# Block sums of a Strassen-type FFN made piece by piece ahead of time, and the last item's rows ordered behind its sums

## Chip, cores, metric

One Trainium2 chip, one core. The metric is the device time of one execution in microseconds (us); three executions of the kernel before were timed, and one more was profiled.

## What is computed

One pre-norm residual layer on x (2048 tokens x 1024 channels, float32). Cut to what matters here:

```python
h = rms_norm(x, mix_norm_g) @ w_in                 # q, k, v, forget gates, z
merged = concat(rms_norm(forgetting_attention(q, k, v, log_f)), rms_norm(spatial_gating(gelu(z))))
x = x + merged @ w_out
xn = rms_norm(x, ffn_norm_g)
gate, up = split(xn @ w_gate_up)                   # 1024 x 2*2816
x = x + (silu(gate) * up) @ w_down                 # 2816 x 1024
out = rms_norm(x, final_norm_g)
```

The change lies in the last three lines, the FFN and the final norm.

## The kernel before

Everything is float32 in and out. To multiply with float32 precision, each operand is split into a high and a low half (a ScalarE cast at L129 and a VectorE subtraction at L132), and each product is three matmuls: high x high, high x low, low x high.

The kernel runs through the input projection, attention with the gating MLP beside it, the output projection, and then the FFN, which starts about 1095 us into the profiled execution. The FFN has five stages: stages 1 and 2 are the up projection (`Up`, gate and up together) for the two halves of the tokens, 22 items each; stages 3, 4 and 5 are the down projection (`Down`) for three ranges of the hidden dimension, 8 items each, an item being 256 tokens. Each item is a two by two block product in the Winograd form: seven products n = 0 to 6 instead of eight. An item's seven left operands are streamed: loaded into `raw` tiles, added and subtracted (L1352, from `stream`) and split into `wh` and `wl` tiles, of which there are six each (`NW`). The seven right operands of a stage stay in place in SBUF for the whole stage, as high and low halves (`R`, some of them stored in tiles that are also named `wh` and `wl`). They are four raw blocks b11, b12, b21, b22 of the right matrix and three block sums made with four additions over 128 x 2048 elements (128 x 1536 in stage 5).

Items are taken in groups of two (`grp`; the last two items of stage 5 are groups of one). In a group, product n of both items runs, then their evacuation (`it.evac(n)`: sums from PSUM into SBUF on VectorE, ScalarE and GpSimd), then n + 1. In the last group of stages 1 to 4, after product n has been done for the last time, the resident operand n is rewritten for the next stage (`refill`, `keep_as`). The four raw blocks of the next stage (`staged`) are loaded ahead into the tiles `sg0` to `sg3`, and the block sums are made in those tiles, by VectorE but for one on GpSimd: one sum before the last group, three within it, between the splits:

```python
        yield keep(0, b11)
        tt(te[1], b11, b11, b12, ALU.add)
        yield keep(1, b11)
        yield keep(2, b21)
        tt(te[2], b21, b21, b11, ALU.subtract)
        tt(te[3], b11, b22, b11, ALU.subtract)
        yield keep(3, b11)
```

In stage 5 an item's two rows of tiles (t = 2 tp and 2 tp + 1) are finished with their last sums: `done` (L1517) squares the row on ScalarE, makes 1/sqrt on VectorE and GpSimd (`rsqrt`, L175 and L177), scales the row on VectorE (L1540) and stores it. These are generators in the list `posts`; the main loop takes a step of the first of them after each product of an item. The last item but for its second row goes a shorter way (t = 14, L1523 to L1533): half of its squares are taken early.

Each engine works its queue in order, and so does SyncE (SP), which issues nearly all loads and stores here. The order in a queue is set when the program is built by a list scheduler: the order of the program is the priority, and what is ready earlier by its own reckoning can go ahead of its place. `with behind(i):` places what is traced in the block after i on i's engine. The loads of attention's first operands are placed in this way after stores of the last chunk of the input projection (L1221 to L1229).

Of the kernel before, what the change touches and what calls it, by code (L numbers as in the profile page):

```python
# [8 lines left out]
F32 = mybir.dt.float32  # L9
F32R = mybir.dt.float32r  # L10
AF = mybir.ActivationFunctionType
ALU = mybir.AluOpType
# [4 lines left out]
P = 128  # L17
S = 2048
D = 1024
# [6 lines left out]
CH = 512  # L26
# [25 lines left out]
KB = [8, 8, 6]  # L52
NF_ = 6
RL = 2
SQ = 'p'
TE = ['vvvv', 'vvpv', 'vvvv', 'vvvv', 'vvvv', 'vvpv']
SE = 'pvpv'
NY = 4
NR = 5
# [27 lines left out]
def trunk(ctx: ExitStack, tc: tile.TileContext, x, x_t, mix_g, w_in, b_f, ln_g, ln_b, w_st, b_st, on_g, w_out,  # L87
# [85 lines left out]
    def rsqrt(p, ss, scale, tag, n=1):  # L173
        a = T(p, [P, n], F32, tag + "a")
        nc.vector.tensor_scalar(a, ss, scale, EPS, ALU.mult, ALU.add)  # L175
        r = T(p, [P, n], F32, tag + "r")
        nc.gpsimd.tensor_tensor(r, a, mhalf[:, 0:n], ALU.pow)  # L177
        return r
# [1149 lines left out]
    def stage():  # L1328
        return [T(pers, [P, 4, CH], F32, f"sg{n}") for n in range(4)]

    def staged(s):

        sg = stage()
        for i, t in enumerate(sg):
            if s < 3:
                ld(t, XT[s - 1][i])
                continue
            kh, r0 = KB[s - 3] // 2, sum(KB[: s - 3])
            r0 = (r0 + (i // 2) * kh) * P
            ld(t[:, 0:kh, :],  # L1340
               w_down[r0 : r0 + kh * P, (i % 2) * CH : (i % 2 + 1) * CH].rearrange("(k p) n -> p k n", p=P))
        return sg

# [5 lines left out]
    JOIN = {2: 0, 6: 3}  # L1349

    def tt(e, o, a, b, op):
        (nc.vector if e == "v" else nc.gpsimd).tensor_tensor(o, a, b, op)  # L1352

    def keep_as(i, src, kh=4):
        rh, rl = resident(i)
        hi_of(nc.scalar, rh[:, 0:kh, :], src)
        lo_of(nc.vector, rl[:, 0:kh, :], src, rh[:, 0:kh, :])
        return rh, rl

    def refill(sg, kh, te):  # L1360

        b11, b12, b21, b22 = (t[:, 0:kh, :] for t in sg)

        def keep(i, src):
            return keep_as(i, src, kh)

        yield keep(0, b11)
        tt(te[1], b11, b11, b12, ALU.add)
        yield keep(1, b11)
        yield keep(2, b21)  # L1370
        tt(te[2], b21, b21, b11, ALU.subtract)
        tt(te[3], b11, b22, b11, ALU.subtract)
        yield keep(3, b11)
        yield keep(4, b12)
        yield keep(5, b21)
        yield keep(6, b22)

    def stream(a11, a12, a21, a22):

# [17 lines left out]
    class Rows:  # L1397
# [10 lines left out]
        def evac(self, n):  # L1408
            ps = self.ps
            if n == 0:  # L1410
                self.x = self.rows()
                for m in range(2):
                    ld(self.x[m], self.source(2 * self.tp + m))
                self.u = T(pev, [P, CH], F32, "u", bufs=NU)
            x = [[self.x[m][:, c * CH : (c + 1) * CH] for c in range(2)] for m in range(2)]
            u = self.u
            if n == 0:
                copies.append(nc.scalar.copy(u, ps[0]))  # L1418
            elif n == 1:
                nc.vector.tensor_tensor(u, u, ps[1], ALU.add)  # L1420
                tt(self.adder, x[0][1], x[0][1], u, ALU.add)
            elif n == 2:
                nc.vector.tensor_tensor(x[0][0], x[0][0], ps[2], ALU.add)
            elif n == 3:
                nc.vector.tensor_tensor(x[1][1], x[1][1], ps[3], ALU.add)
            elif n == 4:
                nc.vector.tensor_tensor(u, u, ps[4], ALU.add)
                tt(self.adder, x[1][1], x[1][1], u, ALU.add)
            elif n == 5:
                nc.vector.tensor_tensor(x[1][0], x[1][0], ps[5], ALU.add)  # L1430
                tt(self.adder, x[1][0], x[1][0], u, ALU.add)
            elif n == 6:
                nc.vector.tensor_tensor(x[0][1], x[0][1], ps[6], ALU.add)
            for m in {5: (1,), 6: (0,)}.get(n, ()):
                posts.append(self.done(2 * self.tp + m, self.x[m], now[0]))

    class Up:
# [17 lines left out]
        def evac(self, n):  # L1455
            ps = self.ps
            if n == 0:
                self.h = T(pev, [P, 2, CH], F32, "hT", bufs=NH)
                self.u = T(pev, [P, CH], F32, "u", bufs=NH)
                self.c = T(pev, [P, CH], F32, "c", bufs=NH)  # L1460
            h0, h1, u, c = self.h[:, 0, :], self.h[:, 1, :], self.u, self.c
            if n == 0:
                nc.scalar.copy(u, ps[0])
            elif n == 1:
                nc.vector.tensor_tensor(u, u, ps[1], ALU.add)
            elif n == 2:
                nc.scalar.activation(h0, ps[2], AF.Silu)
            elif n == 3:
                nc.vector.tensor_tensor(c, u, ps[3], ALU.add)
            elif n == 4:  # L1470
                nc.vector.tensor_tensor(c, c, ps[4], ALU.add)
                nc.vector.tensor_tensor(h1, u, ps[4], ALU.add)
            elif n == 5:
                nc.vector.tensor_tensor(h1, h1, ps[5], ALU.add)
                nc.gpsimd.tensor_tensor(h0, h0, h1, ALU.mult)
            elif n == 6:
                nc.vector.tensor_tensor(u, u, ps[6], ALU.add)
                nc.scalar.activation(h1, u, AF.Silu)
                nc.gpsimd.tensor_tensor(h1, h1, c, ALU.mult)
                kb, r = [(i, j) for i in range(3) for j in range(KB[i])][self.fi]  # L1480
                ld(HD[kb][self.half * 8 : (self.half + 1) * 8, :, r, :].rearrange("b p t -> p b t"),
                   self.h.rearrange("p q (b t) -> p (q b) t", t=P))

    class Down(Rows):
        def __init__(self, kb, tp):
# [14 lines left out]
        def source(self, t):  # L1500
            return XA[t]
# [15 lines left out]
        def done(self, t, xt, at):  # L1517
            if self.kb < 2:
                ld(XA[t], xt)
                return  # L1520
            ss = T(pev, [P, 1], F32, "ss4")
            o = out[t * P : (t + 1) * P, :]
            if t == NB - 2:  # L1523
                right = xt[:, CH:]
                self.squares(right, ss)
                nc.vector.scalar_tensor_tensor(ss, ss, 1.0 / D, self.a, ALU.mult, ALU.add)  # L1526
                r = T(pev, [P, 1], F32, "r4r")
                nc.gpsimd.tensor_tensor(r, ss, mhalf[:, 0:1], ALU.pow)  # L1528
                nc.vector.scalar_tensor_tensor(right, right, r, finb[:, CH:], ALU.mult, ALU.mult)  # L1529
                ld(o[:, CH:], right)  # L1530
                nc.scalar.activation(xt[:, 0:CH], xt[:, 0:CH], AF.Copy, scale=r)
                ld(o[:, 0:CH], xt[:, 0:CH])
# [6 lines left out]
            r = rsqrt(pev, ss, 1.0 / D, "r4")  # L1539
            nc.vector.scalar_tensor_tensor(xt, xt, r, finb, ALU.mult, ALU.mult)  # L1540
            ld(o, xt)
            yield
# [88 lines left out]
    make()  # L1631
    load(1)
    nextR = [None] * 7
    for q in range(len(slots)):
        p, n = slots[q]
        s, i, its, last = grp[p]
        if n == 0 and i == 0 and s > 1:
            R, nextR = nextR, [None] * 7
            if s == 5:
                finb = T(pers, [P, 4, CH], F32, "sg0")[:, 0:2, :].rearrange("p a n -> p (a n)")  # L1640
                ld(finb, fin_g.rearrange("(o n) -> o n", o=1).broadcast_to([P, D]))
        if n == 0 and i == 2 and s < 5:
            sg = staged(s + 1)
        last = last and s < 5
        if n == 4 and s < 5 and i + 2 * len(its) == len(sets[s - 1]):
            b = [t[:, 0 : sets[s][0].kh, :] for t in sg]
            tt(TE[s + 1][0], b[1], b[3], b[1], ALU.subtract)
        if n == 0 and last:
            fill = refill(sg, sets[s][0].kh, TE[s + 1])
        while nq < len(slots) and len(made) + len(grp[slots[nq][0]][2]) <= LW:  # L1650
            make()
        if n == 0:
# [18 lines left out]
                it.evac(m)  # L1671
        if n == 0:
            now[0] = p
        for _ in range(len(its)):
            while posts and next(posts[0], 0) == 0:
                posts.pop(0)
        if last:
            nextR[n] = next(fill)
    finish(posts)
    estk.close()  # L1680

# [43 lines left out]
```

## Time and profile before

| | us |
|---|---|
| median of 3 runs | 2375.95 |
| lowest and highest | 2375.18, 2379.35 |
| profiled execution | 2381.17 |
| its span, first to last instruction | 2379.4 |
| TensorE (PE) busy in the span | 2340.1 |
| VectorE (DVE) busy | 1669.8 |
| ScalarE (ACT) busy | 1055.7 |
| GpSimd (POOL) busy | 623.3 |

The profiled execution is 5.22 us over the median. Sums are made against the profiled execution, and 1.77 us of it lie outside the span. A row of a timeline has the start, the duration, the engine, the line, the operation, the tiles (out <- in) and, in brackets, how long the engine had been idle before it and what ended that. A row of waits has the total, the times and the longest. A row of windows has the length of the window and then the busy time of each engine.

### The profile page before, as it was taken

What the parts mean: (1) busy time and instruction counts of PE and PEld (TensorE: products, weight loads), DVE (VectorE), ACT (ScalarE), POOL (GpSimd) and SP (SyncE); (2) the same over time, 40 slices, a digit from 0 to 9 for tenths busy, and PEclk for the clock granted to TensorE, in tenths of its full rate; (3) what the DMA queues carried; (4) which work ended last, traced back from release to release, by engine and by line L of the source; (5) the groups of instructions that cost most, each with busy time, mean ns of one, the idle gap of its engine ahead of it and who ended that gap; (6) DMA issues with size and microseconds to landing.
All of it is one profiled execution on the core that took longest, in us unless ns stands there. A gap on an engine that the chain in (4) does not pass through costs nothing. (4 is left out here: it accounts for less than half of the span.)

```text
span 2379.4 us, 31425 instructions
## 1 busy us (share of the span) xinstructions
PE 2340.1 (98%) x10582; PEld 1894.4 (80%) x10582; DVE 1669.8 (70%) x2736; ACT 1055.7 (44%) x1770; POOL 623.3 (26%) x705
## 2 busy tenths in 40 slices
PE   9999999999999989999999999999999999999997
PEld 7778777777777768788888888788888878888886
DVE  6658668888888666467655656965555696696888
ACT  5322138777787766344323233432323242332433
POOL 1100012122121222221323323232322325354531
PEclk9999999999999999999999999999999999999999
DMA  8845667655687865666233232423232245455453
GB/s 271 284 154 193 205 206 207 180 161 156 191 211 237 223 206 168 216 214 199 71 89 92 80 94 76 151 83 89 72 89 82 80 141 186 167 186 200 152 190 148
DMA packets 358152, 380.60 MB, mean 160 GB/s; under 512 B 22292, under 2 KB 275924, under 8 KB 355432
## 3 DMA queue, kind: packets, MB, share of 16 engines
q1 hardware_dynamic: 342008, 335.36, 46.6%
q0 software_dynamic: 7616, 27.33, 3.3%
q10 hardware_dynamic: 8368, 15.91, 1.8%
q8 instruction: 85, 1.39, 0.3%
q14 instruction: 75, 0.61, 0.1%
HBM read 253.35 MB, written 125.18 MB: 159 GB/s over the span
## 5 line engine op out<-in xcount | busy, mean ns | idle before, releaser
L129 ACT CAST wh<-raw 128x512 fp32r<-128x512 f32 (+2 forms) x492 | 302.1, 621 | 748.3 <-PE pp L1663 608.3
L132 DVE TENSOR_TENSOR wl<-raw,wh 128x512 fp32r<-128x512 f32 (+2 forms) x496 | 373.2, 762 | 82.0 <-ACT wh L129 81.5
L1663 PE MATMUL pp<-wl,wh 128*128 128x512 f32 x1056 | 325.4, 389 | 1.2 <-ACT u L1418 1.0
L1663 PE MATMUL pp<-wh,wh 128*128 128x512 f32 x1056 | 325.4, 389 | 0.0
L1352 POOL TENSOR_TENSOR raw<-raw 128x512 f32<-128x512 f32 (+1 forms) x124 | 163.6, 1321 | 510.0 <-DMA raw<-in_w_gu_dram 357.9
L132 DVE TENSOR_TENSOR Pl<-Pt,Ph 128x512 fp32r<-128x512 f32 (+1 forms) x320 | 195.2, 615 | 80.4 <-ACT Ph L129 77.5
L1663 PEld LDWEIGHTS pp<-wl,wh 128*128 128x128 f32 x1056 | 198.1, 188 | 43.0 <-ACT u L1418 1.4
L1663 PEld LDWEIGHTS pp<-wh,wh 128*128 128x128 f32 x1056 | 198.2, 188 | 41.2
L738 ACT ACTIVATE Pt<-mx_ps 128x512 f32<-128x512 f32 (+1 forms) x320 | 169.2, 533 | 124.9 <-PE mx_ps L736 120.7
L1663 PE MATMUL pp<-wl,wl 128*128 128x512 f32 x528 | 205.8, 390 | 1.0 <-DVE wl L132 1.0
L1663 PE MATMUL pp<-wh,wl 128*128 128x512 f32 x528 | 205.4, 389 | 0.0
L927 PE MATMUL z<-wh,xz 128*128 128x512 f32 x496 | 188.9, 397 | 0.0
L1352 DVE TENSOR_TENSOR raw<-raw,raw 128x512 f32<-128x512 f32 (+1 forms) x112 | 132.1, 1181 | 77.7 <-POOL raw L1352 74.2
L129 ACT CAST Ph<-Pt 128x512 fp32r<-128x512 f32 (+1 forms) x320 | 175.9, 557 | 19.3 <-PE tp L770 3.8
L363 DVE TENSOR_REDUCE mx<-mx_ps 128x1 f32<-128x512 f32 x192 | 129.9, 682 | 20.5 <-PE mx_ps L361 20.0
L748 POOL TENSOR_SCALAR_AFFINE_SELECT Ph<-Ph 128x128 fp32r<-128x128 f32 x128 | 52.8, 413 | 314.4 <-DVE Pl L132 219.6
L768 PE MATMUL tp<-Ph,V 128*128 128x512 f32 (+1 forms) x320 | 118.8, 371 | 3.7 <-POOL Ph L748 2.6
L735 PE MATMUL mx_ps<-A,D 74*128 74x512 f32 (+1 forms) x320 | 119.3, 373 | 2.9 <-ACT Pt L738 2.9
L361 PE MATMUL mx_ps<-D,A 66*128 66x512 f32 (+2 forms) x320 | 118.6, 373 | 2.6 <-issue 2.0
L773 PE MATMUL tp<-Pl,V 128*128 128x512 f32 (+1 forms) x320 | 118.6, 370 | 1.3 <-POOL Pl L748 0.9
L736 PE MATMUL mx_ps<-B,C 128*128 128x512 f32 (+1 forms) x320 | 117.5, 368 | 0.0
L1663 PEld LDWEIGHTS pp<-wl,wl 128*128 128x128 f32 x528 | 99.1, 188 | 22.6 <-DVE wl L132 2.1
(340 smaller groups left out, 5301.7 us busy)
## 6 DMA issues: line engine op xcount, KB each, us to landing
raw<-in_w_gu_dram SPq DMA_DIRECT2D x88, 512.0 KB
xz<-XS SPq DMA_DIRECT2D x31, 1024.0 KB
HD<-hT SPq DMA_DIRECT2D x44, 512.0 KB
D<-KH SPq DMA_DIRECT2D x112, 128.0 KB
XA<-xa SPq DMA_DIRECT2D x27, 512.0 KB
raw<-HD SPq DMA_DIRECT2D x24, 512.0 KB
XA<-xb SPq DMA_DIRECT2D x21, 512.0 KB
xa<-XA SPq DMA_DIRECT2D x20, 512.0 KB
```

The lines of the kernel that those rows point to most:

```text
L129: return nc.scalar.copy(o, i) if eng is nc.scalar else eng.tensor_copy(o, i)
L132: return eng.tensor_tensor(o, i, f(h), ALU.subtract)
L361: last_mx.append(nc.tensor.matmul(pm[:, 0:n], lhs, Dt[0 : lhs.shape[0], 0:n], start=True, stop=True))
L363: nc.vector.tensor_reduce(mx[:, a, s : s + 1], pm, AX.X, ALU.max)
L735: nc.tensor.matmul(st[:, off:], Dt[:, b * P : (b + 1) * P], A[:, off:], start=True, stop=False)
L736: nc.tensor.matmul(st[:, off:], C[:, b * P : (b + 1) * P], B[:, off:], start=False, stop=True)
L738: nc.scalar.activation(Pt[:, off:], st[:, off:], AF.Exp)
L768: nc.tensor.matmul(pv[:, off:], V[:, 0:P], Ph[:, off:], start=kb == 0, stop=False)
L773: nc.tensor.matmul(pv[:, off:], V[:, 0:P], Pl[:, off:], start=False, stop=kb == 4 * j + 3)
L927: nc.tensor.matmul(pz, xz[a][:, k, :], w[b][:, k, :], start=n == 0, stop=n == 3 * KT - 1)
L1352: (nc.vector if e == "v" else nc.gpsimd).tensor_tensor(o, a, b, op)
L1663: nc.tensor.matmul(pm, a[:, k, :], b[:, k, :], start=on is None and k == 0 and e == 0, stop=k == it.kh - 1 and e == 2, skip_group_check=n ...
```

## The change

The four wide sums of a stage (the table `TE`, the calls in `refill` and the one before the last group) are gone. A generator `block_sums` makes them instead in one piece per group, for 15 groups from the second group of stage 1 on (4 pieces for each of stages 2, 3 and 4, 3 for stage 5): four loads of 128 x 512 into two `xa` tiles after product 3, two VectorE sums after product 5 and two after product 6, and two stores into a DRAM buffer `SM` after product 2 of the next group. Loads and stores stand behind the last store of hidden rows (`hd`) in SP's queue. The resident operands are then loaded ready made: n = 0, 2 and 6 from the source, n = 1, 3, 4 and 5 from `SM`, the first four into `sg0` to `sg3` at item 14 of 22 in stages 1 and 2 and at item 2 of 8 in stages 3 and 4, the other three into `sg0` to `sg2` within the last group, each as soon as the operand that lay there has been split.

In the last group of all, the steps of `posts` are taken two at a time after products 0 to 3, none after 4 and one after 5 and 6, and from product 1 on they are placed behind the item's last sum of that product (`it.last`). The scaling of row 15 is moved behind all of row 14's steps.

The change was described in a few words as "Attention's first operands loaded during the last chunk, together with block sums made a piece per group and the last item's rows behind each product's sums". No line of the diff touches attention or the input projection.

```diff
-TE = ['vvvv', 'vvpv', 'vvvv', 'vvvv', 'vvvv', 'vvpv']
...
+    SM = {s: T(dram, [P, 4, 4, CH], F32, f"SM{s}") for s in (2, 3, 4, 5)}
+    def source(s, n):
+        if n in (0, 2, 6):
+            return block(s, {0: 0, 2: 2, 6: 3}[n])
+        return SM[s][:, {1: 0, 4: 1, 5: 2, 3: 3}[n], 0 : sets[s - 1][0].kh]
+    def fetch(s, n):
+        t = T(pers, [P, 4, CH], F32, f"sg{n % 4}")[:, 0 : sets[s - 1][0].kh]
+        ld(t, source(s, n))
+        return t
+    hd = []
+    def block_sums():
+        last = None
+        for s in (2, 3, 4, 5):
+            for k in range(sets[s - 1][0].kh):
+                n = yield
+                while n != 2:
+                    n = yield
+                if last:
+                    with behind(hd[-1]):
+                        put(*last)
+                while n != 3:
+                    n = yield
+                t = [T(xap, [P, D], F32, "xa") for _ in range(2)]
+                b = [t[i // 2][:, (i % 2) * CH : (i % 2 + 1) * CH] for i in range(4)]
+                with behind(*hd[-1:]):
+                    for i in range(4):
+                        ld(b[i], block(s, i)[:, k])
+                while n != 5:
+                    n = yield
+                tt("v", b[1], b[3], b[1], ALU.subtract)
+                tt("v", b[0], b[0], b[1], ALU.add)
+                n = yield
+                tt("v", b[2], b[2], b[0], ALU.subtract)
+                tt("v", b[3], b[3], b[0], ALU.subtract)
+                last = s, k, t
...
-    def refill(sg, kh, te):
...
+    def refill(s, sg):
+        kh = sets[s - 1][0].kh
+        for n in range(7):
+            r = keep_as(n, sg[n], kh)
+            if n < 3:
+                sg.append(fetch(s, n + 4))
+            yield r
...
             r = rsqrt(pev, ss, 1.0 / D, "r4")
+            if at == len(grp) - 1:
+                yield
             nc.vector.scalar_tensor_tensor(xt, xt, r, finb, ALU.mult, ALU.mult)
...
-        if n == 0 and i == 2 and s < 5:
-            sg = staged(s + 1)
+        if n == 0 and i == max(2, len(sets[s - 1]) - 8) and s < 5:
+            sg = [fetch(s + 1, m) for m in range(4)]
...
-        for _ in range(len(its)):
-            while posts and next(posts[0], 0) == 0:
-                posts.pop(0)
+        tail = p == len(grp) - 1
+        with behind(*[its[0].last] if tail and n else ()):
+            for _ in range((2, 2, 2, 2, 0, 1, 1)[n] if tail else len(its)):
+                while posts and next(posts[0], 0) == 0:
+                    posts.pop(0)
+            if tail and n == 6:
+                next(posts.pop(), None)
         if last:
             nextR[n] = next(fill)
+        if sums and p:
+            try:
+                sums.send(n)
+            except StopIteration:
+                sums = None
```

More of the change, by code (lines that the diff above doesn't have):

```diff
@@ L1329, in stage, with block @@
         return [T(pers, [P, 4, CH], F32, f"sg{n}") for n in range(4)]
+    def block(s, i):
+        if s < 3:
+            return XT[s - 1][i]
+        kh, r0 = KB[s - 3] // 2, sum(KB[: s - 3])
+        r0 = (r0 + (i // 2) * kh) * P
+        return w_down[r0 : r0 + kh * P, (i % 2) * CH : (i % 2 + 1) * CH].rearrange("(k p) n -> p k n", p=P)
     def staged(s):
@@ L1334, in staged, with put @@
         for i, t in enumerate(sg):
[L1335 to L1341, printed above, removed]
-        return sg
+            ld(t, block(s, i))
+        return sg
+    SM = {s: T(dram, [P, 4, 4, CH], F32, f"SM{s}") for s in (2, 3, 4, 5)}
[33 more added lines that the diff above has]
+                last = s, k, t
+        while n != 2:
+            n = yield
+        with behind(hd[-1]):
+            put(*last)
+        yield
+    def put(s, k, t):
+        for a in range(2):
+            ld(SM[s][:, 2 * a : 2 * a + 2, k], t[a].rearrange("p (c n) -> p c n", c=2))
     JOIN = {2: 0, 6: 3}
     def tt(e, o, a, b, op):
-        (nc.vector if e == "v" else nc.gpsimd).tensor_tensor(o, a, b, op)
+        return (nc.vector if e == "v" else nc.gpsimd).tensor_tensor(o, a, b, op)
     def keep_as(i, src, kh=4):
@@ L1358, in keep_as @@
         return rh, rl
-    def refill(sg, kh, te):
[L1362 to L1376, printed above, removed]
+    def refill(s, sg):
[5 more added lines that the diff above has]
+            yield r
     def stream(a11, a12, a21, a22):
@@ L1420, in evac @@
                 nc.vector.tensor_tensor(u, u, ps[1], ALU.add)
-                tt(self.adder, x[0][1], x[0][1], u, ALU.add)
+                self.last = tt(self.adder, x[0][1], x[0][1], u, ALU.add)
             elif n == 2:
-                nc.vector.tensor_tensor(x[0][0], x[0][0], ps[2], ALU.add)
+                self.last = nc.vector.tensor_tensor(x[0][0], x[0][0], ps[2], ALU.add)
             elif n == 3:
-                nc.vector.tensor_tensor(x[1][1], x[1][1], ps[3], ALU.add)
+                self.last = nc.vector.tensor_tensor(x[1][1], x[1][1], ps[3], ALU.add)
             elif n == 4:
                 nc.vector.tensor_tensor(u, u, ps[4], ALU.add)
-                tt(self.adder, x[1][1], x[1][1], u, ALU.add)
+                self.last = tt(self.adder, x[1][1], x[1][1], u, ALU.add)
             elif n == 5:
                 nc.vector.tensor_tensor(x[1][0], x[1][0], ps[5], ALU.add)
-                tt(self.adder, x[1][0], x[1][0], u, ALU.add)
+                self.last = tt(self.adder, x[1][0], x[1][0], u, ALU.add)
             elif n == 6:
-                nc.vector.tensor_tensor(x[0][1], x[0][1], ps[6], ALU.add)
+                self.last = nc.vector.tensor_tensor(x[0][1], x[0][1], ps[6], ALU.add)
             for m in {5: (1,), 6: (0,)}.get(n, ()):
@@ L1480, in evac @@
                 kb, r = [(i, j) for i in range(3) for j in range(KB[i])][self.fi]
-                ld(HD[kb][self.half * 8 : (self.half + 1) * 8, :, r, :].rearrange("b p t -> p b t"),
-                   self.h.rearrange("p q (b t) -> p (q b) t", t=P))
+                hd[:] = [ld(HD[kb][self.half * 8 : (self.half + 1) * 8, :, r, :].rearrange("b p t -> p b t"),
+                            self.h.rearrange("p q (b t) -> p (q b) t", t=P))]
     class Down(Rows):
@@ L1539, in done @@
             r = rsqrt(pev, ss, 1.0 / D, "r4")
+            if at == len(grp) - 1:
+                yield
             nc.vector.scalar_tensor_tensor(xt, xt, r, finb, ALU.mult, ALU.mult)
@@ L1633, in trunk @@
     nextR = [None] * 7
+    sums = block_sums()
+    next(sums)
     for q in range(len(slots)):
@@ L1641, in trunk @@
                 ld(finb, fin_g.rearrange("(o n) -> o n", o=1).broadcast_to([P, D]))
-        if n == 0 and i == 2 and s < 5:
-            sg = staged(s + 1)
+        if n == 0 and i == max(2, len(sets[s - 1]) - 8) and s < 5:
+            sg = [fetch(s + 1, m) for m in range(4)]
         last = last and s < 5
-        if n == 4 and s < 5 and i + 2 * len(its) == len(sets[s - 1]):
-            b = [t[:, 0 : sets[s][0].kh, :] for t in sg]
-            tt(TE[s + 1][0], b[1], b[3], b[1], ALU.subtract)
         if n == 0 and last:
-            fill = refill(sg, sets[s][0].kh, TE[s + 1])
+            fill = refill(s + 1, sg)
         while nq < len(slots) and len(made) + len(grp[slots[nq][0]][2]) <= LW:
```

## The prediction, made blind

> **What bounds the kernel now.** I read the engines' busy times first, then TensorE's waits in the FFN, then windows round the stage ends, then the timelines there and at the kernel's end.
>
> ```profile
> PE 2340.1 (98%) x10582; PEld 1894.4 (80%) x10582; DVE 1669.8 (70%) x2736; ACT 1055.7 (44%) x1770; POOL 623.3 (26%) x705
> ```
>
> TensorE is busy in 98% of the span, so only its waits and what lies after its last matmul can be won. TensorE's waits from 1130 to 2370 us, the whole FFN but its first group:
>
> ```profile
> PE pp L1663 <- DVE wl L132: 4.0, 4, 2.3
> PE pp L1663 <- ACT wh L129: 2.7, 2, 1.4
> PE pp L1663 <- ACT u L1418: 1.0, 1, 1.0
> ```
>
> They are 4.0 + 2.7 + 1.0 = 7.7 us. The windows tell where. Columns: window, length, busy time of PE, PEld, DVE, ACT and POOL with counts, granted clock, DMA share, GB/s.
>
> ```profile
> 1140.00:1480.00 340.00, 340.00 (x1501) 281.53 (x1500) 198.06 (x271) 106.35 (x180) 98.95 (x73) 1.00 0.30 86
> 1480.00:1560.00 80.00, 78.28 (x343) 63.81 (x342) 73.19 (x73) 35.53 (x47) 26.65 (x17) 1.00 0.43 132
> 1900.00:1981.00 81.00, 76.00 (x325) 61.50 (x324) 73.10 (x69) 33.50 (x43) 32.14 (x20) 0.98 0.45 150
> 2060.00:2140.00 80.00, 79.04 (x349) 65.00 (x348) 68.71 (x68) 32.20 (x40) 40.37 (x18) 1.00 0.55 185
> 1955.00:1960.00 5.00, 4.96 (x15) 3.95 (x16) 5.00 (x6) 1.84 (x3) 1.11 (x1) 0.66 0.65 218
> ```
>
> In mid-stage (first row) TensorE never waits, and DVE has 198.06 / 340 = 58% to do. At the end of stage 1 it loses 80 - 78.28 = 1.72 us, of stage 2 81 - 76 = 5.00, of stage 3 80 - 79.04 = 0.96: 7.68, all the waits of the FFN. There DVE is busy for 73.19 of 80 us, 73.10 of 81 and 68.71 of 80, so it is the engine behind. The last row is the stretch behind the longest wait: a clock of 0.66 over 5 us costs (1 - 0.66) x 5 = 1.7 us more. Stage ends cost 9.4 us. How DVE does it, from the timelines of the end of stage 1, with the longest wait (end of stage 2) last:
>
> ```profile
> 1491.11 2.28 DVE L1352 TENSOR_TENSOR sg<-sg,sg 128x2048 f32<-128x2048 f32 x1
> 1503.14 3.16 DVE L1352 TENSOR_TENSOR sg<-sg,sg 128x2048 f32<-128x2048 f32 x1
> 1506.83 2.28 DVE L1352 TENSOR_TENSOR sg<-sg,sg 128x2048 f32<-128x2048 f32 x1
> 1518.83 3.06 DVE L132 TENSOR_TENSOR wh<-sg,wh 128x2048 fp32r<-128x2048 f32 x1
> 1521.81 2.38 DVE L1352 TENSOR_TENSOR raw<-raw,raw 128x512 f32<-128x512 f32 x2
> 1523.67 1.74 ACT L129 CAST wh<-raw 128x512 fp32r<-128x512 f32 x3 [4.13 <-DVE raw L1352]
> 1524.34 0.50 PE L1663 MATMUL pp<-R1h,wh 128*128 128x512 f32 x1 [1.32 <-ACT wh L129]
> 1955.04 0.50 PE L1663 MATMUL pp<-R3h,wl 128*128 128x512 f32 x1 [2.31 <-DVE wl L132]
> ```
>
> The first three rows are block sums in the last group: 2.28 + 3.16 + 2.28 = 7.7 us. DVE then reaches the next group's left operands (1521.81) so late that ScalarE's cast (1523.67) and the matmul (1524.34) wait for them.
>
> The end of the kernel, VectorE's rows, then ScalarE's, TensorE's last and SP's last:
>
> ```profile
> 2359.89 0.68 DVE L1420 TENSOR_TENSOR u<-u,pp 128x512 f32<-128x512 f32 x1
> 2366.52 1.28 DVE L1540 SCALAR_TENSOR_TENSOR sg<-sg,r4r,sg 128x1024 f32<-128x1024 f32 x1 [0.73 <-POOL r4r L177]
> 2367.72 0.68 DVE L1427 TENSOR_TENSOR u<-u,pp 128x512 f32<-128x512 f32 x1
> 2370.37 0.68 DVE L1433 TENSOR_TENSOR sg<-sg,pp 128x512 f32<-128x512 f32 x1
> 2372.60 1.28 DVE L1540 SCALAR_TENSOR_TENSOR sg<-sg,r4r,sg 128x1024 f32<-128x1024 f32 x1 [0.73 <-POOL r4r L177]
> 2373.80 0.15 DVE L1526 SCALAR_TENSOR_TENSOR ss<-ss,a 128x1 f32<-128x1 f32 x1
> 2374.68 0.75 DVE L1529 SCALAR_TENSOR_TENSOR sg<-sg,r4r,sg 128x512 f32<-128x512 f32 x1 [0.73 <-POOL r4r L1528]
> 2370.53 1.06 ACT L1515 ACTIVATE jk<-sg 128x1024 bf16<-128x1024 f32 x1 [4.93 <-issue]
> 2372.25 0.19 ACT L1515 ACTIVATION_READ_ACCUMULATOR jk<-sg 128x1 f32 x1
> 2366.76 0.39 PE L1663 MATMUL pp<-wl,wl 128*128 128x512 f32 x1
> 2375.89 0.38 SPq L1532 DMA_DIRECT2D out_dram<-sg  x1
> ```
>
> TensorE ends at 2366.76 + 0.39 = 2367.15, but VectorE reaches the sum of product 4 (L1427, 2367.72) only after an older row (L1540, 2366.52) that had to wait, and that of product 6 (L1433) ends at 2371.05, 3.9 us after the last matmul.
>
> **The change, part by part.** *Words and diff.* Attention's loads do not change, so the first part of the description is worth 0 and the span up to about 1095 us should repeat.
>
> *Wide sums leave the last groups.* VectorE loses three sums there, 7.7 us at the end of stage 1. The groups, wide sums first, 512-wide sums between SBUF tiles second:
>
> ```profile
> L1352 DVE TENSOR_TENSOR sg<-sg,sg 128x2048 f32<-128x2048 f32 x11 | 27.8, 2528 | 0.0
> L1352 DVE TENSOR_TENSOR sg<-sg,u 128x512 f32<-128x512 f32 x12 | 8.2, 684 | 0.1
> ```
>
> The operands late at 1524.34 were late by 1.32 us and at 1955.04 by 2.31 us. Both are less than 7.7, so with the sums gone the waits should go, and the 0.66 clock with them, since it starts where the wait of 2.31 us ends. What is late next: VectorE still has seven subtractions of about 2.3 to 3.3 us per stage end, so the lead of the left operands still shrinks. That lead (13 us, worked out in the next part) is now used up and overdrawn by 1.3 to 2.3 us; with 7.7 back, some 5 to 6 us remain. Worth: 9.4, the sum of the rows; ends 0 (another wait of the same size comes) and 9.4 (TensorE cannot win more there).
>
> *The sums come back as pieces.* 15 pieces of four 512-wide sums: 4 x 0.684 = 2.7 us of VectorE per group, 41 us in all, where a group of 168 matmuls is 168 x 340 / 1501 = 38.1 us. The cover: VectorE's idle share of 42% is 15.9 us of each group, and ScalarE's casts run ahead of TensorE by all the buffers there are:
>
> ```profile
> ACT wh L129 <- PE pp L1663: 214.8, 117, 2.4
> ```
>
> The casts wait for TensorE to free a `wh` tile (214.8 us in 340): with six tiles and 38.1 / 14 = 2.7 us for each, five stand ready, a lead of some 13 us. I cost the pieces at 0. If that cover were gone, 41 us.
>
> *A wait on VectorE for the pieces' loads.* The first sum of a piece waits for four loads and the queue behind it waits too: evacuations and splits. Nearest rows, VectorE's waits for loads:
>
> ```profile
> DVE xa L1423 <- DMA xa<-XA: 8.0, 4, 3.4
> DVE sg L1352 <- DMA sg<-in_w_down_dram: 1.9, 1, 1.9
> DVE xb L1425 <- DMA xb<-XA: 1.7, 2, 1.4
> ```
>
> The worst is 3.4 us. With the sums, 3.4 + 2.7 = 6.1 per group, less than the 13 of lead. I take 0. Ends: 0 and, with 3.4 in each of 15 groups and no lead, 51.
>
> *SP.* 90 DMAs for pieces and 12 more for operands (28 instead of 16), at 0.38 us to issue (2375.89) some 39 us of SP time over two stages and more. The loads stand behind the last store of hidden rows, and also wait until the stores of the piece before have left the `xa` tiles; a load of weights behind them waits as well. How SP issues weights at a stage end now:
>
> ```profile
> 1495.23 14.87 SPq L1448 DMA_DIRECT2D raw<-in_w_gu_dram  x4
> ```
>
> Four loads over 14.87 us, each as a tile comes free. A wait of 3 to 4 us among them costs part of the lead, nothing of TensorE: 0.
>
> *Fetches in the last group.* Operands 4, 5 and 6 can be loaded once operands 0, 1 and 2 are split. The latest of them:
>
> ```profile
> 1499.28 3.34 DVE L132 TENSOR_TENSOR wl<-sg,wl 128x2048 fp32r<-128x2048 f32 x1
> 1517.62 1.92 ACT L129 CAST wl<-sg 128x2048 fp32r<-128x2048 f32 x1 [3.52 <-PE pp L1663]
> 2120.81 0.38 SPq L1340 DMA_DIRECT2D sg<-in_w_down_dram  x1
> 2128.58 1.76 DVE L1352 TENSOR_TENSOR sg<-sg,sg 128x1536 f32<-128x1536 f32 x1 [1.86 <-DMA sg<-in_w_down_dram]
> ```
>
> The third operand's subtraction ends at 1499.28 + 3.34 = 1502.62, and the seventh is cast at 1517.62: 15.0 us for the load. The nearest price of such a load is the worst in sight: issued at 2120.81 among other traffic, used at 2128.58, 7.8 us, with 1.86 us of VectorE waiting. It fits. Even a wait of 1.86 for each of three (5.6) stays under the 7.7 saved. I take 0; the other end is three waits of 3.4, less 7.7, at four stage ends: 10 us.
>
> *The tail.* In trace the sums are held by rows. Placed behind the sums, rows cannot hold them except by their own length. From L1420 (2359.89) VectorE has ten sums at (2370.37 - 2367.72) / 4 = 0.66, two rows at 2367.72 - 2366.52 = 1.20, and three small steps at 0.15: 6.6 + 2.4 + 0.4 = 9.4, so L1433 would end at 2369.3 instead of 2371.05: 1.75 us. TensorE's end allows 2367.15 + 0.68 = 2367.83: 3.2. Then row 14: its small step (L1526) stood behind row 15 from 2372.25 + 0.19 = 2372.44 to 2373.80. Row 15 now comes behind it: up to 1.36 more. Ends 1.75 and 4.6; I take 2.8, near the lower, since both older rows still have to be done. ScalarE's 2370.53 square of row 15 starts earlier by what the sums gain.
>
> Sum: 9.4 + 2.8 = 12.2. Profiled execution 2381.17 - 12.2 = 2369.0; it stands 5.22 over the median, so the forecast is 2375.95 - 12.2 = 2363.8, 2364.
>
> [...] The half clock sets in right after a wait of 2.31 us and is counted as won. [...] I follow the trace: the windows round the other stage ends show 1.00.
>
> **Rivals.** *Clock stays* (the half clock is not tied to the wait): 1.7 us less, 2365.5. For it: the wait is short beside the slow stretch. Against: the place. [...]
>
> *Part of it comes back.* Fetches of 1 MB meet rows and weights in the last groups, VectorE waits, and one of the two large stage ends keeps its wait: about 5 us less, 2369. If both keep them, the tail alone is left: 2373, the same within measurement. For it: the waits for loads of 3.4 and 1.9 us stand in just such places. Against: 7.7 us of relief.
>
> *Slower: SP.* In each of 15 groups a piece's load waits on its `xa` tiles, and with it the weights behind it in SP's queue, for longer than the lead of 13 us; VectorE in turn waits for the piece. Each microsecond beyond the lead costs TensorE 15. It decides from (12.2 + 4.8) / 15 = 1.1 us per group; at 1.5 us, 2364 + 22 = 2386. Against: no row shows a load that needs more than 7.8.
>
> *The tail fails* (the scheduler puts rows in front all the same): 2.8 less, 2367. The ordering is explicit, so it is in the lower chances of the forecast's own range.
>
> **From the cases to the numbers.** 0.2% is 4.8 us, about what a measurement of this kernel can tell from no change. All waits go, with or without the half clock and with a tail between its ends: 0.68, giving 2361 to 2367 (12.2 + 1.8 at best; 12.2 - 1.7 - 1.1 and a little at worst); 0.14 of the 0.68 is for the clock that stays. One stage end keeps its wait: 0.16, 2367 to 2371. Both keep theirs: 0.08, 2371 to 2377. Slower through SP: 0.05. Better than 2361: 0.03. Faster by more than 0.2% (below 2371.2) 0.87, within 0.08, slower 0.05. The range 2360 to 2371 holds 0.84 or so.
>
> **What would show it.** Right: no waits of TensorE for `wl` and `wh` at the stage ends; the window round the end of stage 2 about 6 us shorter for the same matmuls, with a clock of 1.00; wide sums on `sg` gone from VectorE's groups and 60 sums on `xa` in their place; in the mid-stage window DVE 2.7 us per group higher and TensorE still without idle time; L1427 and L1433 within 2 us of their products' ends, L1526 before the last L1540. Wrong: VectorE or ScalarE waiting for `xa` or `sg` loads for more than about 8 us in one group, SP's weights issued later than now against their group, or L1433 again 3 us and more behind the last matmul.

## The result

The changed kernel takes 2369.49 us (median of 8 runs, 2365.97 to 2372.74) against 2376.97 us before (8 runs, 2371.74 to 2379.35). The ratio is 0.9972, 95% interval 0.9962 to 0.9983: faster by 0.28%, or 7.5 us, where 12.2 us were forecast. The time is inside the range of 2360 to 2371 and 5.5 us above the point of 2364. The profiled execution took 2371.31 us, with a span of 2369.2.

First the busy times, from the page, then TensorE's waits in the FFN from 1130 to 2370 us (total, times, longest):

```profile
PE 2335.3 (99%) x10582; PEld 1893.5 (80%) x10582; DVE 1674.3 (71%) x2781; ACT 1056.6 (45%) x1770; POOL 611.8 (26%) x704
```

```profile
PE pp L1709 <- ACT u L1508: 3.3, 1, 3.3
PE pp L1709 <- ACT u L1463: 1.0, 1, 1.0
PE pp L1709 <- DVE wl L131: 0.7, 1, 0.7
```

Of the 6.7 us that TensorE waited for `wl` and `wh`, 0.7 is left. The wait of 1.0 for `u` was there before; it stands in every kernel below, so it has nothing to do with the wide sums. One of 3.3 us is new, and it is the largest of all. The windows of the changed kernel, in the columns of those before (window, length, busy time of PE, PEld, DVE, ACT, POOL, clock, DMA share, GB/s):

```profile
1140.00:1480.00 340.00, 340.00 (x1501) 281.53 (x1500) 219.37 (x305) 105.25 (x178) 99.49 (x72) 1.00 0.49 144
1480.00:1560.00 80.00, 80.00 (x354) 66.24 (x353) 63.54 (x72) 32.94 (x44) 23.91 (x14) 1.00 0.68 217
1900.00:1981.00 81.00, 79.31 (x349) 65.02 (x348) 68.48 (x70) 34.94 (x45) 33.70 (x23) 1.00 0.60 206
2060.00:2140.00 80.00, 80.00 (x355) 66.24 (x354) 65.95 (x70) 33.57 (x42) 32.03 (x21) 1.00 0.70 248
1560.00:1570.00 10.00, 6.68 (x24) 5.05 (x24) 7.22 (x8) 4.86 (x9) 5.45 (x5) 0.88 0.30 85
```

At the three stage ends TensorE now loses 0, 1.69 and 0 us instead of 1.72, 5.00 and 0.96, and the end of stage 2 runs at a clock of 1.00. VectorE has 219.37 - 198.06 = 21.3 us more in mid-stage, 2.4 per group, without any wait of TensorE. The last row is the new loss: 3.32 us, and a clock of 0.88 over 10 us, 1.2 more inside the window. It lies after the end of stage 1, at the second group of stage 2: 2082 matmuls of 168 to a group are recorded before it, which is 12.4 groups, and stage 1 has 11.

From the first matmul of the FFN to its last are 1267.84 us, where it was 1271.59: 3.75 won. From the end of the last matmul to the end of the span are 9.28 instead of 12.28: 3.0 won. The rest of the span's 10.2 us, 3.4, lies ahead of the FFN (its first matmul starts at 1092.12 instead of 1095.56), where no line has changed. It is the spread between two executions: in all 14 profiled kernels, none of which changes a line ahead of the FFN, it starts between 1089.70 and 1095.56, and the kernel before happens to be the latest. So 6.75 us can be put down to the change in the profiles; the medians are 7.5 apart.

Why TensorE waits at 1566.47, from the timelines of VectorE, SP, ScalarE and TensorE, in that order:

```profile
1533.36 1.89 DVE L131 TENSOR_TENSOR wl<-raw,wh 128x512 fp32r<-128x512 f32 x3
1543.17 0.69 DVE L1406 TENSOR_TENSOR xa<-xa,xa 128x512 f32<-128x512 f32 x1 [7.92 <-DMA xa<-in_w_down_dram]
1544.51 0.68 DVE L1514 TENSOR_TENSOR c<-u,pp 128x512 f32<-128x512 f32 x1
1545.10 1.74 DVE L131 TENSOR_TENSOR wl<-raw,wh 128x512 fp32r<-128x512 f32 x1
...
1564.03 0.68 DVE L1522 TENSOR_TENSOR u<-u,pp 128x512 f32<-128x512 f32 x1
...
1528.81 2.06 SPq L1526 DMA_DIRECT2D HD<-hT  x2
1530.93 1.94 SPq L1395 DMA_DIRECT2D SM<-xa  x2
1532.96 1.23 SPq L1356 DMA_DIRECT2D sg<-in_w_down_dram  x1
1535.31 2.82 SPq L1378 DMA_DIRECT2D xa<-in_w_down_dram  x4
1538.22 11.42 SPq L1493 DMA_DIRECT2D raw<-in_w_gu_dram  x4
...
1564.80 0.63 ACT L1523 ACTIVATE hT<-u 128x512 f32<-128x512 f32 x1 [3.71 <-DVE u L1522]
1565.84 0.58 ACT L1508 COPY u<-pp 128x512 f32<-128x512 f32 x1
...
1566.47 0.72 PE L1709 MATMUL pp<-wl,wh 128*128 128x512 f32 x2 [3.32 <-ACT u L1508]
```

This is the first group of stage 2. SP issues the piece's loads only from 1535.31 on, behind the stores of the hidden rows (1528.81) and of the piece before (1530.93) and the load of an operand (1532.96). VectorE's next instruction is the piece's first sum, and it stands still for 7.92 us, to 1543.17. Behind it in VectorE's queue stand an evacuation (L1514) and the splits `wl<-raw,wh`, which free the `raw` tiles for the next weights. SP therefore issues four weight loads over 11.42 us, the splits and sums of the next item come late, and so does the sum of the group's last product for `u`, at 1564.03. ScalarE gets only at 1565.84 to the copy that frees an accumulator for the second group, and TensorE has been idle for 3.32 us.

### The profile page after: what moved, and what is told of

It is laid out like the page before. It is cut to its first block, busy times and chain, and to the rows that moved or that the text cites. A ratio compares the mean times of both kernels' runs of the same rounds, so it can differ in the third digit from the quotient of the medians.

```text
span 2369.2 us, 31668 instructions
## 1 busy us (share of the span) xinstructions
PE 2335.3 (99%) x10582; PEld 1893.5 (80%) x10582; DVE 1674.3 (71%) x2781; ACT 1056.6 (45%) x1770; POOL 611.8 (26%) x704
## 5 line engine op out<-in xcount | busy, mean ns | idle before, releaser
L1406 POOL TENSOR_TENSOR raw<-raw 128x512 f32<-128x512 f32 (+1 forms) x124 | 172.1, 1389 | 568.9 <-DMA raw<-in_w_gu_dram 337.1
```

The lines of the kernel that those rows point to most:

```text
L1406: return (nc.vector if e == "v" else nc.gpsimd).tensor_tensor(o, a, b, op)
```

## The experiments

Ratios are to the kernel before, with 95% intervals. The edits stand against the changed kernel, but that of the tail alone against the kernel before, and those on top of late sums against that kernel. The runs of this section come from three chips, each with its own runs of the kernel before, so kernels are best compared by their ratios.

**The tail alone.** The kernel before, with the new order of the last group and nothing else:

```diff
+            if at == len(grp) - 1:
+                yield
             nc.vector.scalar_tensor_tensor(xt, xt, r, finb, ALU.mult, ALU.mult)
...
+        tail = p == len(grp) - 1
+        with behind(*[its[0].last] if tail and n else ()):
+            for _ in range((2, 2, 2, 2, 0, 1, 1)[n] if tail else len(its)):
...
```

> The kernel before with only the new order of the last group (steps of the rows behind the sums, row 15's scaling last); wide block sums stay. The stage ends keep their waits (7.7 us of TensorE waits in the FFN). From TensorE's last matmul to the end of the span: 12.2 us before, 9.2 in the changed kernel, so 3.0 us less are expected here, a ratio of 0.9987 to the kernel before. If the tail's gain needs the rest of the change (sums further ahead at the end of the FFN), it is under 1 us, 0.9996 or more.

Measured: 2374.24 against 2375.99 us, ratio 0.9996 (0.9987 to 1.0004). In the profile the stretch after the last matmul falls to 9.22 us, 3.1 less, and the waits at the stage ends stay (VectorE's `wl` 2.4 us, ScalarE's `wh` 2.2). The time alone doesn't resolve 3 us here: its ratio is the one expected of a tail that gains next to nothing, and its interval reaches to the other. The one profile shows the gain.

**The sums alone.** The pieces and the ready operands, with the old order of the tail (the two edits above taken back).

> The changed kernel with the old order of the last group: pieces and ready-made operands only. From the first FFN matmul (L1709) to the last the changed kernel takes 3.8 us less than the kernel before, since 9.4 us of waits and half clock at the old stage ends go and a new wait of 3.3 us with a half clock behind it (5.2 us) comes at about 1566 us. So a ratio of 0.9984 is expected, with the same wait at the second group of stage 2. If that wait were chance of one execution, it is missing here and the ratio is 0.996.

Measured: 2371.46 us, 0.9979 (0.9970 to 0.9988). The new wait is here too, with 2.04 us at 1563.60, and 11.12 us follow the last matmul. So it comes with the pieces, not with the tail.

**No piece in the first group of stage 2.**

```diff
-        if sums and p:
+        if sums and p and p != 11:
```

> The changed kernel, with the pieces paused in the first group of stage 2 (that piece and those after it come one group later). Theory one, VectorE waits in order for that piece's loads where the lead is still thin: the wait at about 1566 us and its half clock go, 5.2 us less than the changed kernel, ratio to the kernel before 0.995. Theory two, SP issues the weights of the next group too late because of the piece's DMAs: goes as well (this run does not tell them apart, the next does). Theory three, the wait is left over from the stage end (seven wide splits) and has nothing to do with the piece: it stays, 0.997.

Measured: 2364.29 us, 0.9953 (0.9941 to 0.9965). TensorE's waits from 1130 us on:

```profile
PE pp L1709 <- ACT u L1463: 1.0, 1, 1.0
```

The wait is gone, and the time falls by 5.2 us in the medians, 4.5 by the ratios. VectorE's waits in the other groups are still there:

```profile
L1406 DVE TENSOR_TENSOR xa<-xa,xa 128x512 f32<-128x512 f32 x45 | 30.9, 689 | 65.9 <-issue 29.7 <-DMA xa<-in_w_down_dram 22.4 <-DMA xa<-XT 13.4
```

65.9 us of VectorE standing still cost TensorE nothing in mid-stage. Nor does the longest wait of the changed kernel, 8.26 us before its sum at 1618.16, two groups further on in stage 2.

**No piece in a group of mid-stage**, as a control: the same edit with the sixth group of stage 1 (`p != 5`).

> Control of skip_first: the changed kernel with the pieces paused in the sixth group of stage 1 instead of the first group of stage 2. If it is the piece in the first group of stage 2 that matters, the wait near 1566 us stays (2 to 3.3 us and perhaps a half clock): 0.997 to 0.998. If any pause helps, by making one wait fewer for VectorE, 0.995.

Measured: 2369.68 us, 0.9976 (0.9967 to 0.9985). The wait stays, 2.76 us at 1565.04 with a half clock behind it (a matmul starts every 0.43 us there, and every 0.227 in mid-stage). It is the place of the pause that counts.

**Late sums.** The piece keeps its place and its loads; its four sums come behind the last product's evacuation.

```diff
-                while n != 5:
+                while n != 6:
                     n = yield
-                tt("v", b[1], b[3], b[1], ALU.subtract)
-                tt("v", b[0], b[0], b[1], ALU.add)
-                n = yield
...
+                with behind(ev[0]):
+                    tt("v", b[1], b[3], b[1], ALU.subtract)
+                    tt("v", b[0], b[0], b[1], ALU.add)
...
             elif n == 6:
-                nc.vector.tensor_tensor(u, u, ps[6], ALU.add)
+                ev[:] = [nc.vector.tensor_tensor(u, u, ps[6], ALU.add)]
```

> The changed kernel with loads and stores of the pieces as they are, but a piece's four sums placed on VectorE behind the last product's evacuation of the group, some 10 us later. Theory one (VectorE stands waiting for the piece's loads, 3.4 to 8.3 us in each of 15 groups, 77 us in all): VectorE's waits for xa go, the wait at 1566 us and its half clock go, ratio 0.995. Theory two (SP's order delays the weights): SP's order is hardly changed, so the wait at 1566 us stays, 0.997. Theory three (left over from the stage end): stays, 0.997.

Measured: 2364.30 us, 0.9954 (0.9942 to 0.9966). The piece's sums in VectorE's groups from 1100 to 2290 us, first of the changed kernel, then with late sums (count | busy, mean ns | idle before them):

```profile
L1406 DVE TENSOR_TENSOR xa<-xa,xa 128x512 f32<-128x512 f32 x45 | 30.8, 689 | 77.5 <-DMA xa<-in_w_down_dram 46.5 <-issue 17.1 <-DMA xa<-XT 13.4
```

```profile
L1406 DVE TENSOR_TENSOR xa<-xa,xa 128x512 f32<-128x512 f32 x45 | 31.7, 731 | 0.0
```

These are 45 of the 60 sums, with the same loads, and they no longer wait: 77.5 us are gone. TensorE's waits with late sums:

```profile
PE pp L1709 <- ACT u L1463: 1.0, 1, 1.0
PE pp L1709 <- DVE wl L131: 0.8, 1, 0.8
PE pp L1709 <- DVE sg L1470: 0.2, 1, 0.2
```

SP's queue shows the way it went. Its waits for VectorE's splits from 1500 to 1570 us, the changed kernel first, then late sums:

```profile
SPq L1493 <- DVE wl L131: 10.8, 4, 7.3
```

```profile
SPq L1493 <- DVE wl L131: 4.7, 5, 1.8
```

The weights waited for VectorE's splits for up to 7.3 us, and for up to 1.8 without the sum in front of them (and 3.1 once for an evacuation). SP's last weight load for the second group is issued, counted from the first matmul of the FFN, after 457.5 us in the changed kernel, 456.8 in sums alone, 457.4 with the pause in mid-stage and 457.5 with the fetch held back (below): the four kernels that have the wait. In the ten that don't, it is issued after 445.7 to 453.0.

The run does not tell the first two theories apart as cleanly as was expected. Without VectorE's earlier waits the whole stage end comes sooner: the hidden rows are stored 432.3 us after the first matmul of the FFN, 436.7 in the changed kernel, and this lead would also cover a delay by SP's order. Skipping the piece (436.4) takes away its loads and its sums together. The trace of the changed kernel gives both a share: beside the kernel without the piece, the first weight load is issued 3.9 us later, behind the piece's transfers, and the last 11.2 us later, with 7.3 us of waiting for VectorE's split in between.

**Late sums and no piece in the first group**, both edits together.

> Late sums and no piece in the first group of stage 2, the tail as in the changed kernel. all_three had it with row 14 first and kept a wait of 0.96 us at the end of stage 2, so pausing gives nothing beyond late sums: 0.9953, the same as either alone, and the tail 0.9 us shorter than in all_three (8.9).

Measured: 2363.32 us, 0.9954 (0.9940 to 0.9967), the same as either alone. So both take away the same wait, and no larger one lies behind it. All three kernels beat the changed kernel, by some 5 to 6 us in their medians and 4 to 5 by the ratios; late sums is the simplest that keeps a piece in every group.

**The operands' fetch held back.** The four 1 MB loads of the next stage's operands, placed behind a store of hidden rows, so that they don't run beside them:

```diff
-            sg = [fetch(s + 1, m) for m in range(4)]
+            with behind(*hd[-1:]):
+                sg = [fetch(s + 1, m) for m in range(4)]
```

> The changed kernel with the first four operand loads of stages 2 and 3 placed in SP's queue behind the last store of hidden rows before item 14, so that the 1 MB load issued at 1533 us, just ahead of the piece's loads, comes some 300 us later. If that load is what makes VectorE wait 7.9 us for the piece instead of about 5, VectorE's wait there falls to 5 or 6 us, and TensorE's wait at the second group of stage 2 from 3.3 to 1 us or less, without the half clock: 0.995 to 0.996 of the kernel before. If the late store of hidden rows alone (1528.8 us) sets it, the wait stays at 2 us and more: 0.997.

Measured: 2371.68 against 2375.14 us, 0.9990 (0.9980 to 1.0000). VectorE still waits for the piece:

```profile
1544.53 0.69 DVE L1406 TENSOR_TENSOR xa<-xa,xa 128x512 f32<-128x512 f32 x1 [6.62 <-DMA xa<-in_w_down_dram]
```

6.62 instead of 7.92 us. The hidden rows are stored at 1532.09 here, still just ahead of the piece's loads, TensorE waits 2.38 us at 1569.69, two new waits of 0.7 appear, and that of 0.73 at the end of stage 2 is gone. The expected 1 us or less did not come: the 1 MB loads are at most a small part of the cause.

**Wide operations put back**, to test the main term: on top of late sums, three operations 2048 wide on `sg1` and `sg3` that leave the values as they are.

```diff
         for n in range(7):
+            for m in ((), (1,), (), (3, 3))[n] if n < 4 else ():
+                tt("v", sg[m], sg[m], sg[m], ALU.max)
             r = keep_as(n, sg[n], kh)
```

> The kernel with the late sums (0.9954 of the kernel before), to which three wide VectorE operations (maximum of a tile with itself, which changes nothing) are added in each last group where the wide sums stood, some 2.3 to 3.2 us each. If it is VectorE's load in the last group that made TensorE wait at the stage ends, the waits at about 1524, 1946 and 1953 us come back, 6 us and more of them (with a half clock or without): 0.998 to 0.999. If it was something else that the change moved (the order of loads, ready-made operands), the stage ends stay without waits but for 0.8 us: 0.9955.

Measured: 2363.68 us, 0.9953 (0.9941 to 0.9966), no change. The scheduler had placed the wide operations well ahead of the last groups, so this says nothing on the stage ends. It does say something on the first group of stage 2: three of them stand there, from 1533.25 to 1542.35, 6.9 us of VectorE's time with splits and evacuations between them, and TensorE does not wait. So time lost on VectorE in that group is not enough by itself; the changed kernel loses its 7.92 us in one piece, after waits in the groups before.

**The same, each placed behind the split before it**, so that they stay in the last group:

```diff
-        lo_of(nc.vector, rl[:, 0:kh, :], src, rh[:, 0:kh, :])
+        kept[:] = [lo_of(nc.vector, rl[:, 0:kh, :], src, rh[:, 0:kh, :])]
...
             for m in ((), (1,), (), (3, 3))[n] if n < 4 else ():
+                with behind(*kept):
+                    tt("v", sg[m], sg[m], sg[m], ALU.max)
```

> The kernel with the late sums and three wide VectorE operations added in each last group (maximum of a tile with itself, which changes nothing), this time pinned behind the subtraction of the operand before, so that they stand where the wide sums stood: one before operand 1's split, two between those of operands 2 and 3. In the kernel wide_back they stood unpinned, and the scheduler moved them ahead of the last group, so its time says nothing on the stage end. If VectorE's load in the last group is what made TensorE wait at the stage ends, some 6 us of waits near 1520 and 1940 to 1960 us come back, 0.998 of the kernel before. If not, 0.9955.

Measured: 2374.26 against 2374.65 us, 0.9995 (0.9987 to 1.0004): the gain is gone. VectorE's three rows at the end of stage 1, then TensorE's waits from 1130 us on:

```profile
1486.58 2.28 DVE L1406 TENSOR_TENSOR sg<-sg 128x2048 f32<-128x2048 f32 x1
1497.06 2.79 DVE L1406 TENSOR_TENSOR sg<-sg 128x2048 f32<-128x2048 f32 x1
1500.37 2.28 DVE L1406 TENSOR_TENSOR sg<-sg 128x2048 f32<-128x2048 f32 x1
```

```profile
PE pp L1714 <- ACT wh L128: 3.0, 2, 1.7
PE pp L1714 <- DVE wl L131: 2.4, 4, 1.0
PE pp L1714 <- ACT u L1468: 1.0, 1, 1.0
```

The waits for `wh` and `wl` are back at all three stage ends, and two stretches of half clock with them (a matmul every 0.43 us from 1520.80 and from 1943.93). The FFN takes 1272.15 us, with late sums 1262.61 and with the same operations unpinned 1261.71: 9.5 us or more for some 7.4 us of VectorE's time at the end of stage 1, and about as much at the ends of stages 2 and 3.

**Row 14 first.** On top of late sums, all that is left of row 15 placed behind row 14's small step:

```diff
-                nc.vector.scalar_tensor_tensor(ss, ss, 1.0 / D, self.a, ALU.mult, ALU.add)
+                r14.append(nc.vector.scalar_tensor_tensor(ss, ss, 1.0 / D, self.a, ALU.mult, ALU.add))
...
-    finish(posts)
+    with behind(*r14):
+        finish(posts)
```

> The kernel with the late sums and, at the end, row 15's scaling placed behind row 14's small step on VectorE. The prediction counted up to 1.36 us for this order, which the changed kernel does not have (its small step runs after the scaling, at 2363.55). Row 14's square root then starts 1.3 us sooner, but the two scalings still follow each other on VectorE: from TensorE's last matmul to the end 8.9 becomes 8.0 (0.8 to 0.9 us less), a ratio of 0.995, not to be told from 0.9954 by the time alone. If the end is set by the stores, it stays at 8.9.

Measured: 2365.18 us, 0.9958 (0.9946 to 0.9971). 9.78 us follow the last matmul, 8.87 with late sums alone: a miss. VectorE's last steps, then SP's last stores:

```profile
2357.11 0.16 DVE L1571 SCALAR_TENSOR_TENSOR ss<-ss,a 128x1 f32<-128x1 f32 x1 [0.60 <-ACT jk L1560]
2357.24 1.28 DVE L1587 SCALAR_TENSOR_TENSOR sg<-sg,r4r,sg 128x1024 f32<-128x1024 f32 x1
2358.97 0.75 DVE L1574 SCALAR_TENSOR_TENSOR sg<-sg,r4r,sg 128x512 f32<-128x512 f32 x1 [0.44 <-POOL r4r L1573]
```

```profile
2359.71 0.33 SPq L1577 DMA_DIRECT2D out_dram<-sg  x1
2360.14 0.39 SPq L1588 DMA_DIRECT2D out_dram<-sg  x1
2360.61 0.41 SPq L1575 DMA_DIRECT2D out_dram<-sg  x1
```

The order of the steps is the one wanted, and VectorE ends 4.88 us after the last matmul instead of 5.23. But row 15's whole store (L1588, 512 KB) is now issued between the last two stores of row 14. The last store is issued no sooner, and from the end of its issue to the end of the span there are 3.6 us instead of 2.8. That this store is what makes the end late is read from this order; no run tests it.

**All three**: late sums, no piece in the first group, row 14 first.

> Late sums, no piece in the first group of stage 2, and row 14 first. Late sums alone keep a wait of 0.83 us at the end of stage 2 that the kernel without a piece in that group does not have. So 0.8 us less from this and 0.8 from the tail: 0.9947, at or under the best so far (0.9953).

Measured: 2366.63 us, 0.9960 (0.9947 to 0.9972), with 9.79 us after the last matmul: a miss, with the same order of the stores (2360.03, 2360.45, 2360.93). The wait at the end of stage 2, expected to go, is 0.96 us here.

**Late sums with the old tail.**

> Late sums with the old order of the last group: the price of the tail beside a quiet stage end. From TensorE's last matmul to the end 11.1 to 12.3 us instead of 8.9: 2.2 to 3.4 us more than late_sums, a ratio of 0.9963 to 0.9968. If the tail's order is worth no more than the time of the kernel with the tail alone showed (1.0 us), 0.9958.

Measured: 2363.42 us (2360.53 to 2368.87), 0.9956 (0.9943 to 0.9970). 10.70 us follow the last matmul, 1.8 more than with the new tail; the times don't tell the two apart (0.9956 and 0.9954), and the expected 0.9963 to 0.9968 did not come. In time, the worth of the tail stays open; the profiles give it as 1.8 to 3.1 us.

## Why the forecast was right, and where it was not

**The direction and its main term held.** "Wide sums leave the last groups" was priced at 9.4 us. In the two kernels without the new wait the FFN is 9.0 (late sums) and 10.0 us (no piece in the first group of stage 2) shorter than before, and with wide operations put back in their place it is 9.5 us longer. That VectorE's wide sums caused the waits is thus shown. That the sizes agree so well is in part luck, for the make-up differs. The 9.4 count as won the 0.97 us for `u`, which no kernel wins, and all of the waits for `wl`, of which 0.73 us stays in the changed kernel; they leave out what the idle times of the rows don't show (last section); and the 9.5 contain two stretches of half clock where the kernel before has one.

**The step that failed is "A wait on VectorE for the pieces' loads ... I take 0".** Two of its numbers were wrong. The wait was taken as at most 3.4 us, from loads that SP had issued in good time; measured were 77.5 / 15 = 5.2 us on the mean and 8.3 at worst:

```profile
DVE xa L1406 <- DMA xa<-in_w_down_dram: 46.5, 8, 8.3
DVE xa L1406 <- DMA xa<-XT: 13.4, 3, 4.9
```

And the cover was taken as 13 us in each of 15 groups. It is that in mid-stage, where such waits cost nothing. But the prediction's own paragraph on the wide sums had left only 5 to 6 us of it, by its estimate, at a stage end, and the first group of stage 2 starts there. A wait of 7.92 us does not fit into 5 to 6, and even the 6.1 us per group that the prediction allowed hardly does. The two paragraphs were never put side by side. The estimate is a rough one: VectorE's wait there is 7.92, 7.94, 8.49 and 6.62 us in the four kernels that have it, and TensorE's wait 3.32, 2.04, 2.76 and 2.38.

The price here: 3.32 us of wait, and a stretch of half clock right behind it. The clock is 0.89, 0.50 and 0.76 in the three windows of 2 us from 1566 on, which costs (0.11 + 0.50 + 0.24) x 2 = 1.7 more: 5.0. The forecast missed by 5.5, and two kernels without this wait stand at 2364.3 and 2364.3, the forecast's 2364; to the microsecond that is luck, as the make-up of the 9.4 shows. Skipping the piece in one group, or moving all its sums behind the evacuation, each brings it; one skipped elsewhere does not. That the piece in the first group of stage 2 is the cause is thus shown from both sides. That it works through VectorE's queue is shown by the trace, with 7.3 of the 11.2 us by which the weights are late; the share of SP's order, 3.9 us, no run takes away alone. Nothing behind the sum starts before it: the evacuation L1514 starts 452.4 us after the FFN's first matmul, 442.7 where the piece is skipped and 443.8 where its sums come later. ScalarE's rows of the changed kernel show the same: the copy of 1565.84 takes a product whose matmuls had all started by 1557.56, into a `u` that was last read at 1559.94, but it stands behind L1523, for which ScalarE was idle for 3.71 us.

**The tail's size was right and its make-up wrong.** Forecast 2.8 us, between 1.75 for the sums alone and 4.6 with all of row 14's 1.36; profiled 3.0. VectorE's rows of the changed kernel's end:

```profile
2357.46 0.68 DVE L1472 TENSOR_TENSOR u<-u,pp 128x512 f32<-128x512 f32 x1
2360.11 0.68 DVE L1478 TENSOR_TENSOR sg<-sg,pp 128x512 f32<-128x512 f32 x1
2362.34 1.29 DVE L1587 SCALAR_TENSOR_TENSOR sg<-sg,r4r,sg 128x1024 f32<-128x1024 f32 x1 [0.73 <-POOL r4r L176]
2363.55 0.15 DVE L1571 SCALAR_TENSOR_TENSOR ss<-ss,a 128x1 f32<-128x1 f32 x1
2364.43 0.75 DVE L1574 SCALAR_TENSOR_TENSOR sg<-sg,r4r,sg 128x512 f32<-128x512 f32 x1 [0.73 <-POOL r4r L1573]
```

TensorE ends at 2359.96. The sum of product 6 (L1478) ends at 2360.79, 0.83 behind it instead of 3.9: 3.1 us, all of the gain. With the pieces and the old order (sums alone) it ends 2.69 behind, so here the new order is worth 1.9 of the 3.1, near the 1.75 worked out for the sums; the other 1.2 are there without it, and the forecast had no term for them. Row 14's small step (L1571) still follows row 15's scaling (L1587), where "L1526 before the last L1540" was forecast: 0 instead of up to 1.36. Row 14 first shows that in the form tried this step is not worth it. That 2.8 comes out is therefore luck in part.

**The rivals.** *Clock stays* is refuted by its own case: the stretch at the end of stage 2 left with its wait, and came back with the waits in the kernel with wide operations. That the wait is short, the point in its favour, counts for little: with wide operations placed, the half clock from 1520.80 on, a matmul every 0.43 us, comes right after waits of 1.74 and 0.36 us. *Part of it comes back* (2369) gave the size of what was measured, but by another way: not the fetches in the last group, but the piece in the next. Its 2369 is right by accident. *Slower by SP* named the right queue, the weights behind the piece's loads, and put it in all 15 groups; it decided in one. Of the signs named in advance, "VectorE ... waiting for `xa` ... for more than about 8 us in one group" and "SP's weights issued later" are the ones that came; but the wait of more than 8 us (8.26 at 1618.16) did no harm, and the harmful one, 7.92, was under that mark.

## What to carry to other kernels

A cover is to be counted group by group: what a stage end has used up is not there in the group after it, and where a wait of 8.26 us was free in one group, one of 7.92 cost 5 us in another. The sum that waited there takes 0.69 us itself; its price came from its place in VectorE's queue, ahead of work on the critical path. It belongs behind the work that is due, and that move alone won 4 to 5 us here. To test a suspected load on an engine, pin the extra work where it is suspected: unpinned, the scheduler moved it to where it was free.

## What was not expected of the hardware

Half clock does not go by the length of a wait alone. The granted clock was 0.52 from 1957 to 1959 us before and 0.50 from 1568 to 1570 in the changed kernel; in the other kernels half clock is read from matmuls that start every 0.43 us instead of every 0.227. It followed waits of 1.22 + 0.36 us (tail alone, at 1945.2), 1.29 + 0.36 and 1.74 + 0.36 (wide operations placed), 2.31 (before), 2.76 (pause in mid-stage) and 3.32 (the changed kernel), and did not follow 1.32 + 0.36 and 1.35 + 0.36 (before, 1524 and 1946) and 2.04 (sums alone): in the kernel before the clock is 1.00 from 1524 to 1530 and from 1946 to 1950, and in sums alone a matmul starts every 0.23 us behind the wait. What decides between them, the runs don't show.

At the one place worked out here, a wait cost TensorE more than the idle time that its row shows: 1.59 us against 1.32. The matmuls of the kernel before on both sides of its first wait, whose own row starts at 1524.34:

```profile
1522.64 0.39 PE L1663 MATMUL pp<-wh,wl 128*128 128x512 f32 x1
...
1524.68 0.40 PE L1663 MATMUL pp<-R1l,wh 128*128 128x512 f32 x1
```

In a run of them one starts every 0.227 us (340 / 1501). From 1522.64 to 1524.68 are 2.04 us, where two starts take 0.45: 1.59 are lost, and the row of 1524.34 shows 1.32. That is 0.27 more; at as much for each of the seven waits of the FFN from 1130 us on it is an estimated 1.9 us before, which no sum of idle times contains.
